# Feed-forward products of a two-layer decoder step: from one product in seven parts to both, with the squares kept in DRAM

## The chip, the cores and the metric

One core of a Trainium2 chip runs the whole program. The metric is the device time of one launch in microseconds (us), the median over the runs.

## The reference

Two layers work on 1056 tokens (1024 of a prompt, 32 of eight sampled sequences) with model width 1024. Layer 0 mixes tokens with a gated product over chunks of 128 positions, layer 1 with a sparse attention (an indexer, the top keys of each query, softmax). Each layer ends with a feed-forward net (FFN) of width 4096:

```python
def sqrelu_mlp(h, w1, w2):
    a = jax.nn.relu(h @ w1)
    return (a * a) @ w2
...
        xp = xp + op
        xs = xs + os_
        xp = xp + sqrelu_mlp(rms_norm(xp, norm_ffn[i]), ffn_w1[i], ffn_w2[i])
        xs = xs + sqrelu_mlp(rms_norm(xs, norm_ffn[i]), ffn_w1[i], ffn_w2[i])
```

In `dsa_sample`, each of the eight sequences attends to 1024 cached keys, gathered by pages, and to its own four new ones.

## The kernel before

Every fp32 operand is kept as two reduced fp32 parts, high and low, and every product is three matmuls: high by high, high by low, low by high (`mm3`, lines L242 to L248). `split` (L203, L204) makes the parts: ScalarE rounds the high one, VectorE (or GpSimd, where `lo_w` says so) subtracts for the low one. A scheduler places the instructions on each engine in advance; tiles come from pools whose `bufs` says how many buffers a name turns over.

The mixer ends with `out_proj`, which adds a product to the residual `X`, held in SBUF for the whole FFN (L500), and writes the scaled and split input of the FFN into the hidden state `h0`, `h1`, `h2` (L206, L207), chunk by chunk of 384, 384 and 288 tokens.

The FFN goes through the 4096 hidden columns in 16 blocks of 256. The first product of a block is plain: two weight tiles, each 24 matmuls for each of the three chunks. VectorE applies relu and the norm's factor (L526), ScalarE squares (L539). The second product takes tokens in two pairs of quarters (264 tokens each) and forms a 2 by 2 by 2 block product with seven products instead of eight: GpSimd adds and subtracts the squared hidden quarters (`combine0`, `combine1`, L550 to L558) and the weight blocks (L568 to L571), `split` makes `A2` and `w`, and `w2_pair` runs seven products for each of four output pairs and both token pairs, 168 matmuls of 264 columns for a block (L590 to L592). Every product is added into `X` at once, on VectorE from PSUM, and for one of the seven on GpSimd through a copy (L603, L581). The last of the 16 blocks uses a plain second product, and adds into `X` at L643.

The order follows this: `ffn` emits the first product of the next block between the four output pairs of the current one, and the scheduler keeps TensorE supplied from both.

## Time and profile before

| what | value |
|---|---|
| median of 3 runs | 2438.83 us (2437.76 to 2439.71) |
| the profiled execution | 2439.28 us, of it a span of 2436.9 us |
| granted TensorE clock, mean | 0.982 |
| TensorE busy | 2336.8 us, 96% of the span |
| VectorE, ScalarE, GpSimd busy | 69%, 44%, 54% |
| bytes moved by DMA | 158.38 MB, mean 65 GB/s |

Busy time of TensorE is the time in which a matmul is under way, and matmuls overlap; the spacing of their starts tells how fast it runs. A group's idle time is what its engine waited ahead of it, followed by what ended most of that wait.

### The profile page before, as it was taken

The numbers are of one execution on the slowest core, as the hardware profiler recorded it, in microseconds if no ns is written. First come the engines' busy times: TensorE is split into PE (matmuls) and PEld (weight loads), VectorE is DVE, ScalarE is ACT, GpSimd is POOL, SyncE is SP. The second block draws the span as 40 slices with busy tenths as digits, with TensorE's granted clock in tenths as the row PEclk, the third lists the DMA queues.
The fourth block names the chain that finished last, engine by engine and source line by source line (L and its number), as shares of the span: only waits on it lengthen the run. The fifth ranks groups of instructions, "written<-read, shape, count | busy, mean of one in ns | idle before, by whom it ended". The sixth has DMA issues, their size and how long they took to land.

```text
span 2436.9 us, 42780 instructions
## 1 busy us (share of the span) xinstructions
PE 2336.8 (96%) x15961; PEld 2246.2 (92%) x15961; DVE 1692.9 (69%) x3732; ACT 1062.5 (44%) x2164; POOL 1310.4 (54%) x1695
## 2 busy tenths in 40 slices
PE   8999999999999999989988968999999999999998
PEld 7999999999999999988988747899999999999998
DVE  6151257777777777774998879735677777777775
ACT  6232243333333333355865767734333333333335
POOL 2245446676676676561224435414566766766754
PEclk9999999999999999999999979999999999999999
DMA  6211301111111111141223441040111111111111
GB/s 231 61 46 35 123 27 46 47 48 49 44 48 48 49 52 40 55 131 30 84 70 104 142 173 27 10 158 27 44 48 45 48 49 45 51 46 49 53 44 72
DMA packets 180800, 158.38 MB, mean 65 GB/s; under 512 B 10376, under 2 KB 169712, under 8 KB 179568
## 3 DMA queue, kind: packets, MB, share of 16 engines
q1 hardware_dynamic: 176496, 136.78, 18.0%
q0 software_dynamic: 4096, 18.88, 2.3%
q8 instruction: 125, 2.05, 0.4%
q14 instruction: 83, 0.68, 0.1%
HBM read 134.15 MB, written 21.47 MB: 64 GB/s over the span
## 4 chain that ended last, share of the span: by engine, by line
PE 35%; DVE 9%; POOL 4%; issue 4%; ACT 2%; DMA 1%; SPq 0%; another core or an unknown queue 0%; DVEq 0%; POOLq 0%; ACTq 0%
PE ps L242 4%; PE ps L248 4%; PE ps L247 3%; PE px L242 3%; PE px L248 3%; PE px L247 3%; PE ps L590 2%; PE ps L591 1%; PE ps L592 1%; DVE sc L895 1%; POOL st L558 1%; PE pt L1138 1%; PE pt L592 1%; PE pt L591 1%; PE pt L590 1%
## 5 line engine op out<-in xcount | busy, mean ns | idle before, releaser
L581 POOL TENSOR_TENSOR X<-X,scr 128x264 f32<-128x264 f32 x480 | 427.0, 913 | 165.0 <-DVE X L581 119.4
L248 PE MATMUL ps<-h,w 128*128 128x384 f32 (+1 forms) x1344 | 438.3, 326 | 1.6 <-POOL w L204 1.4
L242 PE MATMUL ps<-h,w 128*128 128x384 f32 (+1 forms) x1344 | 437.1, 325 | 0.7 <-DVE scr L909 0.4
L247 PE MATMUL ps<-h,w 128*128 128x384 f32 (+1 forms) x1344 | 435.8, 324 | 0.0
L203 ACT ACTIVATE w<-raw 128x1024 fp32r<-128x1024 f32 (+2 forms) x248 | 250.6, 1012 | 305.6 <-PE px L247 123.3
L204 DVE TENSOR_TENSOR w<-raw,w 128x1024 fp32r<-128x1024 f32 (+1 forms) x211 | 298.4, 1414 | 32.9 <-ACT w L203 32.6
L242 PE MATMUL px<-h,w 128*128 128x384 f32 (+1 forms) x960 | 310.8, 324 | 0.3
L248 PE MATMUL px<-h,w 128*128 128x384 f32 (+1 forms) x960 | 309.8, 323 | 0.0
L247 PE MATMUL px<-h,w 128*128 128x384 f32 (+1 forms) x960 | 309.2, 322 | 0.0
L603 ACT ACTIVATE scr<-ps 128x264 f32<-128x264 f32 x240 | 92.7, 386 | 426.4 <-PE ps L592 380.3
L248 PEld LDWEIGHTS ps<-h,w 128*128 128x128 f32 x1344 | 254.4, 189 | 3.1 <-POOL w L204 1.7
L242 PEld LDWEIGHTS ps<-h,w 128*128 128x128 f32 x1344 | 254.6, 189 | 2.4 <-ACT w L203 1.0
L247 PEld LDWEIGHTS ps<-h,w 128*128 128x128 f32 x1344 | 254.4, 189 | 0.6
L581 DVE TENSOR_TENSOR X<-X,ps 128x264 f32<-128x264 f32 x480 | 197.4, 422 | 64.3 <-PE ps L592 64.3
L581 DVE TENSOR_TENSOR X<-X,px 128x264 f32<-128x264 f32 x480 | 194.2, 422 | 52.2 <-PE px L592 52.2
L581 DVE TENSOR_TENSOR X<-X,pt 128x264 f32<-128x264 f32 x480 | 203.1, 423 | 33.7 <-PE pt L592 29.0
L590 PE MATMUL ps<-A,w 128*128 128x264 f32 x720 | 206.8, 288 | 20.2 <-ACT A L203 20.2
L591 PE MATMUL ps<-A,w 128*128 128x264 f32 x720 | 206.6, 290 | 7.6 <-DVE A L204 7.5
L592 PE MATMUL ps<-A,w 128*128 128x264 f32 x720 | 203.6, 284 | 0.0
L568 POOL TENSOR_TENSOR raw<-raw 128x128 f32<-128x128 f32 x120 | 56.6, 472 | 267.7 <-DMA raw<-in_ffn_w 178.1
L204 DVE TENSOR_TENSOR A<-st,A 128x264 fp32r<-128x264 f32 (+2 forms) x184 | 164.1, 905 | 45.7 <-ACT A L203 45.6
L242 PEld LDWEIGHTS px<-h,w 128*128 128x128 f32 x960 | 180.4, 188 | 1.3 <-DVE X L581 1.2
...
## 6 DMA issues: line engine op xcount, KB each, us to landing
...
```

Of the source, the lines that this page charges most:

```text
L203: S.activation(hi, src, AF.Copy)
L204: (lo_w[0] or V).tensor_tensor(lo, src, f(hi), op=ALU.subtract)
L242: PE.matmul(out, lh, rh, start=first, stop=False)
L247: PE.matmul(out, lh, rl, start=False, stop=False)
L248: PE.matmul(out, ll, rh, start=False, stop=last)
L558: G.tensor_tensor(q[:, 1], q[:, 2], q[:, 1], op=ALU.subtract)
L568: G.tensor_tensor(sm[0], a21, a22, op=ALU.add)
L581: eng.tensor_tensor(x, x, src, op=op)
L590: PE.matmul(p, wh, xh, start=first, stop=False, skip_group_check=not first)
L591: PE.matmul(p, wh, xl, start=False, stop=False, skip_group_check=not first)
L592: PE.matmul(p, wl, xh, start=False, stop=True, skip_group_check=not first)
L603: S.activation(u, p, AF.Copy)
```

## The change

Both products of the FFN use the seven-product scheme, over eight blocks of 512 hidden columns (`NB`), in two phases. `out_proj` no longer keeps `X`: it streams rows of the residual from DRAM and back, and writes the scaled input into `XG`, in two halves of 528 tokens. `combos` makes and splits seven combinations of each half (14 in all) into slots that take the memory of the closed hidden state. Phase 1 runs 16 steps (`fb`, `kk`) of 168 matmuls of 264 columns; `summed` puts the outputs into a tile `h` (ScalarE writes four, VectorE adds four for each half), and `squares` applies relu, squares, makes the combinations for the second product, and stores 1.08 MB to DRAM (`hd`) for each half. Phase 2 reads them back (`hidden`), and for each of 8 blocks and four output pairs `m` runs 84 matmuls of 264 columns; the sums of 7 blocks go to the residual in DRAM by an accumulating DMA on GpSimd's queue, those of the last block into rows read back. The sample attention handles four sequences at a time for its softmax and masks from PSUM, without a copy of the mask.

```diff
+    def out_proj(w, gain, pre, x_in, x_out):
+        sx = [ExitStack() for _ in range(3)]
+        XG = [None, pool("x1", sx[1]).tile([P, NK, TH], F32, name="xg1")]
+        XG[0] = pool("x0", sx[0]).tile([P, NK, TH], F32, name="xg0")
+        rp = pool("xr", sx[2])
...
+            rows[d] = rp.tile([P, T], F32, name="row", bufs=3)
...
+            x = rows[o][:, sl]
+            V.tensor_tensor(x, p, x, op=ALU.add)
+            sumsq(x, o, sl)
+            for pr in range(2):
+                a, b = max(sl.start, pr * TH), min(sl.stop, (pr + 1) * TH)
+                if a < b:
+                    S.activation(XG[pr][:, o, a - pr * TH:b - pr * TH], rows[o][:, a:b], AF.Copy, scale=gain[:, o:o + 1])
+            if c == NC - 1:
+                SP.dma_start(x_out[o // 2][o % 2], rows[o])
...
+    def wino(nk, wt, xt, pr, post):
+        banks = {}
+        for key, first in PRODS:
+            if first:
+                banks[key[0]] = ps({"u": "ps", "v": "px"}.get(key[0], "pt"))
+            p = banks[key[0]][:, :SN]
+            kw = dict(skip_group_check=not first)
+            for k in range(nk):
+                wh, wl, xh, xl = wt(key, 0, k), wt(key, 1, k), xt(key, pr, 0, k), xt(key, pr, 1, k)
+                PE.matmul(p, wh, xh, start=first and k == 0, stop=False, **kw)
+                PE.matmul(p, wh, xl, start=False, stop=False, **kw)
+                PE.matmul(p, wl, xh, start=False, stop=k == nk - 1, **kw)
+            post(key, p)
+            yield
...
+    def run(*blocks):
+        for _ in PRODS:
+            for g in blocks:
+                next(g)
...
+    def summed(outs, add=False):
...
+        def start(p, q, op=ALU.add):
+            if add:
+                V.tensor_tensor(outs[q], outs[q], p, op=op)
+            else:
+                S.activation(outs[q], p, AF.Copy)
...
+        def post(key, p):
+            if key == "v5":
+                start(p, 3)
+            elif key == "u1":
+                start(p, 0)
+            elif key == "v3":
+                v3.append(p)
+            elif key == "u6":
+                start(p, 1)
+                V.tensor_tensor(outs[1], v3[0], outs[1], op=ALU.add)
+            elif key == "q4":
+                start(p, 2, ALU.subtract)
+            elif key == "p2":
+                V.tensor_tensor(outs[0], p, outs[0], op=ALU.add)
+            else:
+                V.tensor_tensor(outs[2], p, outs[2], op=ALU.add if add else ALU.subtract)
+                V.tensor_tensor(outs[3], p, outs[3], op=ALU.add)
+        return post
...
+    def w_sums(sm, a11, a21, a12, a22):
+        s1, s2, s4, s3 = sm
+        G.tensor_tensor(s1, a21, a22, op=ALU.add)
+        G.tensor_tensor(s2, s1, a11, op=ALU.subtract)
+        G.tensor_tensor(s4, a12, s2, op=ALU.subtract)
+        G.tensor_tensor(s3, a11, a21, op=ALU.subtract)
...
+    def w1_block(w1, fb, kk):
+        r = [raw([P, 2, 4, P]) for _ in range(2)]
+        for h in range(2):
+            for z in range(2):
+                c0 = fb * 512 + z * 256 + kk * P
+                SP.dma_start(r[h][:, z], w1[h * 512:(h + 1) * 512, c0:c0 + P].rearrange("(k p) f -> p k f", p=P))
...
+        sm = [raw([P, 2, 4, P]) for _ in range(2)]
+        s1, s2, s4, s3 = (sm[z // 2][:, z % 2] for z in range(4))
+        w_sums((s1, s2, s4, s3), a11, a21, a12, a22)
+        wt = {}
+        for key, src in (("v5", s1), ("u1", a11), ("v3", s4), ("u6", s2), ("q4", a22), ("p2", a12), ("u7", s3)):
+            wt[key] = wslot([P, 2, 4, P])
+            split(wt[key][:, 0], wt[key][:, 1], src)
+        return lambda key, z, k: wt[key][:, z, k]
...
+    def w2_block(w2, fb, m):
+        r, sm = raw([P, 2, 2, 2, P]), raw([P, 4, 2, P])
+        for h in range(2):
+            for z in range(2):
+                r0, c0 = fb * 512 + h * 256, m * 256 + z * P
+                SP.dma_start(r[:, h, z], w2[r0:r0 + 256, c0:c0 + P].rearrange("(k p) f -> p k f", p=P))
+        w_sums([sm[:, z] for z in range(4)], *(r[:, z // 2, z % 2] for z in range(4)))
+        wt = {}
+        for keys, src in ((("v5", "u6"), sm[:, 0:2]), (("u1",), r[:, 0, 0:1]), (("v3", "u7"), sm[:, 2:4]),
+                          (("p2", "q4"), r[:, 1])):
+            t = wslot([P, 2, 2, 2, P])
+            split(t[:, 0, :len(keys)], t[:, 1, :len(keys)], src)
+            for z, key in enumerate(keys):
+                wt[key] = t[:, :, z]
+        return lambda key, z, k: wt[key][:, z, k]
+    def ffn(layer, XG, sx, x_acc, done, keep):
...
+        def combos(pr, homes):
+            b11, b12, b21, b22 = (XG[pr][:, 4 * i:4 * i + 4, j * SN:(j + 1) * SN] for i in range(2) for j in range(2))
+            t1, t2, t3, t4 = (raw([P, 4, SN]) for _ in range(4))
+            def put(key, src, eng=None):
+                t = HC[pr][key] = homes[key]([P, 2, 4, SN])
+                lo_w[0] = eng
+                split(t[:, 0], t[:, 1], src)
+                lo_w[0] = None
...
+            put("v5", t1)
+            put("u1", b11)
+            put("v3", b22, G)
+            V.tensor_tensor(t3, b22, b12, op=ALU.subtract)
+            V.tensor_tensor(t2, t3, b11, op=ALU.add)
+            put("u6", t2)
+            V.tensor_tensor(t4, t2, b21, op=ALU.subtract)
+            put("q4", t4)
+            put("p2", b21, G)
+            put("u7", t3)
...
+        def squares(h, fb, kk, pr):
+            c = h[:, 0:4].rearrange("p (i j) t -> p i (j t)", i=2)
+            rb = rbc[:, None, pr * TH:(pr + 1) * TH].to_broadcast([P, 2, TH])
+            V.scalar_tensor_tensor(c, c, 0.0, rb, op0=ALU.max, op1=ALU.mult)
+            S.activation(c, c, AF.Square)
+            G.tensor_tensor(h[:, 4:8:2], h[:, 1:4:2], h[:, 0:2], op=ALU.subtract)
+            G.tensor_tensor(h[:, 5], h[:, 6], h[:, 0], op=ALU.add)
+            G.tensor_tensor(h[:, 7], h[:, 5], h[:, 2], op=ALU.subtract)
+            SP.dma_start(hd[fb][:, :, kk, pr].rearrange("j p t -> p j t"), h)
...
+        for fb in range(NB):
+            for kk in range(2):
+                wt = w1_block(w1, fb, kk)
+                hh = [fp.tile([P, 8, SN], F32, name="h", bufs=2) for _ in range(2)]
+                blocks = [wino(4, wt, xt1, pr, summed([hh[pr][:, q] for q in range(4)])) for pr in range(2)]
+                if fb == kk == 0:
...
+        def hidden(fb, some):
+            for key in some:
+                t = A2[fb, key] = homes[fb % 2][key]([P, 2, 2, 2, SN])
+                r = raw([P, 2, 2, SN])
+                SP.dma_start(r, hd[fb][HID[key]])
+                split(t[:, 0], t[:, 1], r)
...
+        for fb in range(NB - 1):
+            for m in range(4):
+                wt = w2_block(w2, fb, m)
+                out = fp.tile([P, 2, T], F32, name="out", bufs=2)
+                run(*(block(fb, m, pr, wt, out) for pr in range(2)))
+                G.dma_start(out=x_acc[m].rearrange("o p t -> p o t"), in_=out, accum_op=ALU.add)
...
+            wt = w2_block(w2, fb, m)
+            fetch(m)
+            run(*(block(fb, m, pr, wt, X[m], True) for pr in range(2)))
+            for i in range(2):
+                done(X, 2 * m + i, slice(0, T), c8)
+        wts = {m: w2_block(w2, fb, m) for m in (2, 3)}
...
+    def sample_softmax(z):
+        sel = cst("sel")[SB, z * P:(z + 1) * P]
+        mx = bl.tile([P, 3], F32, name="mxs", bufs=2)
...
+            V.tensor_tensor_reduce(out=SS[z][:, c0:c1], in0=p[:, :c1 - c0], in1=SS[z][:, c0:c1], scale=-ATTN_SCALE,
+                                   scalar=mx[:, i - 1:i] if i else 3.4e38, op0=ALU.add, op1=ALU.min,
+                                   accum_out=mx[:, i:i + 1])
...
+            vgs.append(c8([P, 2048], F32))
...
-    sample_mask()
-    for kv in range(2):
-        sample_softmax(kv)
```

In the sample attention the score dots move into each sequence's key loop, the mask product is made for each group of four and added straight from PSUM, and the values are gathered into the FFN's slots before the softmax.

The scheduler's order shows what this moves. First, ScalarE where layer 0's FFN begins: before, the last rows are the scaled input of the last chunk (`h2`) with the weights `w` among them, and then the first squares (`st`).

```order
L206 ACTIVATE h2_71<-X_2516,gains_78 128x288 [waits PE_49] x3
L203 ACTIVATE w_3584<-raw_3578 128x1024 [waits DMAHW3_49,PE_49]
L299 ACTIVATE scr_3320<-X_2516 128x288 [waits DVE_49,Pool_49]
L206 ACTIVATE h2_71<-X_2516,gains_78 128x288 [waits PE_49]
L539 ACTIVATE st_3391<-scr_3389 128x264 [waits DVE_49]
```

The same place of the changed kernel, ScalarE: `c` are the split combinations (the last one made ahead is `c_3455`), `w` the first weights of phase 1.

```order
L220 ACTIVATE c_3416<-raw_3399 128x1056 [waits DVE_49,PE_49]
L220 ACTIVATE c_3419<-xg0_2536 128x1056 [waits Activation_49]
L220 ACTIVATE c_3422<-raw_3398 128x1056
...
L220 ACTIVATE c_3449<-raw_3432 128x1056 [waits DVE_49]
L220 ACTIVATE c_3452<-xg1_2532 128x1056
L220 ACTIVATE c_3455<-raw_3431 128x1056
L220 ACTIVATE w_3474<-raw_3468 128x512 [waits Pool_49]
L220 ACTIVATE w_3477<-raw_3462 128x512 [waits DMAHW7_49]
```

All 14 splits of combinations stand before the first weight, and the first of them waits for TensorE. VectorE's rows have the same order: 10 low parts ahead of `w_3474`.

Second, GpSimd in the middle of phase 1, changed kernel: L682 to L684 are the combinations of the squares in a tile `h`, L600 to L603 the sums of weight blocks.

```order
L682 TENSOR_TENSOR h_4929<-h_4929 128x2x264 [waits DMAHW3_49,Activation_49]
L602 TENSOR_TENSOR raw_5381<-raw_5375,raw_5380 128x512 [waits DMAHW4_49,DVE_49]
L603 TENSOR_TENSOR raw_5381<-raw_5374 128x512
L683 TENSOR_TENSOR h_4929<-h_4929 128x264 [waits Pool_49]
L684 TENSOR_TENSOR h_4929<-h_4929 128x264 [waits Pool_49]
L600 TENSOR_TENSOR raw_5619<-raw_5613,raw_5614 128x512 [waits DMAHW3_49,DMAHW0_49,DVE_49]
L682 TENSOR_TENSOR h_4930<-h_4930 128x2x264 [waits DMAHW6_49,Activation_49]
L601 TENSOR_TENSOR raw_5619<-raw_5619,raw_5613 128x512 [waits DMAHW7_49,Pool_49]
L683 TENSOR_TENSOR h_4930<-h_4930 128x264 [waits Pool_49]
L684 TENSOR_TENSOR h_4930<-h_4930 128x264 [waits Pool_49]
```

Sums of weights stand between the combinations of a tile, which its store to DRAM waits for. ScalarE then starts the next tile of that half with a row that waits for that store (a DMA):

```order
L577 ACTIVATE h_5168<-px_5170 128x264 [waits DMAHW1_49,Activation_49,Pool_49]
L577 ACTIVATE h_5168<-ps_5198 128x264
L577 ACTIVATE h_5168<-pt_5278 128x264
L681 ACTIVATE h_4930<-h_4930 128x1056 [waits DVE_49]
L577 ACTIVATE h_5168<-ps_5198 128x264 [waits PE_49]
```

Third, ScalarE in phase 2, changed kernel: `out` is the tile of sums, which L727 on GpSimd's queue accumulates into DRAM. The first write of a tile waits for that DMA (DMASW) of the tile two back.

```order
L577 ACTIVATE out_7631<-px_7632 128x264 [waits DMASW0_49,DVE_49,PE_49]
L577 ACTIVATE out_7631<-px_7640 128x264 [waits PE_49]
L577 ACTIVATE out_7631<-ps_7648 128x264 [waits PE_49]
L220 ACTIVATE w_7770<-raw_7751 128x512 [waits DMAHW3_49,DMAHW2_49,PE_49]
L577 ACTIVATE out_7631<-ps_7656 128x264 [waits PE_49]
```

The wait is on the accumulate of `out_7347`, issued at L727, two tiles earlier.

## Rows read from the trace of the kernel before

**Rows 1.** The page, part 1: busy time of each engine.

```profile
PE 2336.8 (96%) x15961; PEld 2246.2 (92%) x15961; DVE 1692.9 (69%) x3732; ACT 1062.5 (44%) x2164; POOL 1310.4 (54%) x1695
```

**Rows 2.** Windows: two stretches; busy time and count by engine, granted clock, DMA share, GB/s.

```profile
341.00:1040.00 699.00, 684.57 (x4822) 677.76 (x4822) 526.92 (x1039) 254.02 (x525) 452.72 (x593) 1.00 0.16 47
...
1695.00:2437.00 742.00, 720.79 (x5074) 713.53 (x5072) 549.81 (x1086) 282.36 (x584) 473.28 (x619) 1.00 0.16 49
```

**Rows 3.** One line's instructions, with the first and the last start.

```profile
L500 DVE TENSOR_TENSOR X<-ps,X x24: 444/548/559, 263.8 to 1694.9; 128x384 f32<-128x384 f32 x16, 128x288 f32<-128x288 f32 x8
...
L653 SPq DMA_DIRECT2D xd<-X x24: 319/320/731, 1046.2 to 1074.0; - x24
...
L643 DVE TENSOR_TENSOR X<-px,X x24: 442/545/558, 1045.7 to 2424.3; 128x384 f32<-128x384 f32 x16, 128x288 f32<-128x288 f32 x8
```

**Rows 4.** Timeline of TensorE in layer 1: start, length, line, operation.

```profile
1866.82 0.29 PE L590 MATMUL pt<-A,w 128*128 128x264 f32 x1
...
1867.91 0.34 PE L242 MATMUL ps<-h,w 128*128 128x384 f32 x1
1868.09 0.34 PE L247 MATMUL ps<-h,w 128*128 128x384 f32 x1
```

**Rows 5.** The chain that ended last, layer 1: start, length, what.

```profile
1857.72 1.71 POOL st L556
...
1902.83 1.71 POOL st L556
```

**Rows 6.** Groups by line and shape: count, busy us, mean ns, idle before.

```profile
L203 ACT ACTIVATE w<-raw 128x1024 fp32r<-128x1024 f32 x220 | 233.1, 1060 | 290.0 <-PE px L247 123.3 <-PE ps L591 72.2 <-POOL raw L571 37.5
L204 DVE TENSOR_TENSOR w<-raw,w 128x1024 fp32r<-128x1024 f32 x203 | 290.5, 1431 | 32.9 <-ACT w L203 32.6 <-issue 0.3
L204 POOL TENSOR_TENSOR w<-raw,w 128x1024 fp32r<-128x1024 f32 x17 | 41.7, 2458 | 83.9 <-ACT w L203 83.9
L204 POOL TENSOR_TENSOR w<-raw,w 128x512 fp32r<-128x512 f32 x20 | 26.2, 1320 | 77.5 <-ACT w L203 69.5 <-DVE idh L470 7.8
L204 DVE TENSOR_TENSOR raw<-pt,raw 128x512 fp32r<-128x512 f32 x76 | 51.6, 685 | 24.4 <-ACT raw L203 16.7 <-PE px L247 5.9 <-issue 1.7
L603 ACT ACTIVATE scr<-ps 128x264 f32<-128x264 f32 x240 | 92.7, 386 | 426.4 <-PE ps L592 380.3 <-POOL X L581 46.1
L581 DVE TENSOR_TENSOR X<-X,px 128x264 f32<-128x264 f32 x480 | 194.2, 422 | 52.2 <-PE px L592 52.2
L413 DVE SCALAR_TENSOR_TENSOR GV<-GV,mv,gain_bc 128x1024 f32<-128x1024 f32 x8 | 10.2, 1277 | 0.0
```

**Rows 7.** Timelines of GpSimd and VectorE, 1811 to 1814 us.

```profile
1811.85 0.76 POOL L558 TENSOR_TENSOR st<-st 128x264 f32<-128x264 f32 x1
1812.56 1.75 POOL L556 TENSOR_TENSOR st<-st 128x264 f32<-128x264 f32 x1
...
1811.75 0.76 DVE L581 TENSOR_TENSOR X<-X,px 128x264 f32<-128x264 f32 x2
1812.43 1.26 DVE L204 TENSOR_TENSOR w<-raw,w 128x1024 fp32r<-128x1024 f32 x1
```

**Rows 8.** DMA issues: count, median us from issue to landing.

```profile
raw<-in_cache_k,idh POOLq DMA_INDIRECT x16, 5.2
...
h<-in_cache_v,idh POOLq DMA_INDIRECT x8, 6.2
```

**Rows 9.** Timeline of TensorE, sample attention.

```profile
1406.18 0.28 PE L247 MATMUL px<-KT,t 128*128 128x256 f32 x1
1406.30 0.28 PE L248 MATMUL px<-KT,t 128*128 128x256 f32 x1
...
1410.22 0.58 PE L242 MATMUL px<-KT,t 128*128 128x256 f32 x1 [3.41 <-DVE mx L1125]
1410.59 0.42 PE L247 MATMUL px<-KT,t 128*128 128x256 f32 x1
1410.81 0.41 PE L242 MATMUL px<-KT,t 128*128 128x256 f32 x1
```

435 lines of the change are left out of this document (185 added, 250 removed).

## The prediction

> **What bounds the kernel now.** I read the page's busy times first: TensorE is busy 96% of the span, the other engines 44% to 69% [rows 1], so what counts is how many matmuls there are, how long one takes, and where TensorE waits. The windows give the stage: in 699 us of layer 0's FFN TensorE is busy 684.6 us, in layer 1's 742 us with the tail 720.8 us, at full clock both times, with DMA at 0.16 of its engines [rows 2]. The FFN of layer 0 lasts from about 341 to 1074 us, 733 us; that of layer 1 from 1694.9 to the last add at 2424.3, with the add itself about 729.5 us [rows 3]. Together 1462 of 2439 us.
>
> For the price of a matmul, the spacing of starts serves, not the length shown, since matmuls overlap: nine of 264 columns take 1867.91 - 1866.82 = 1.09 us, 0.121 us each, and one of 384 columns 0.18 (0.455 ns a column) [rows 4]. A block of 256 hidden columns has 144 matmuls of 352 columns on average (0.160 us) and 168 of 264: 23.0 + 20.3 = 43.4 us. The chain of waits passes the same GpSimd sum every 45.1 us [rows 5], so a block waits some 1.7 us, 26 us over a layer.
>
> **What the change saves.** Before, a layer has 2304 first-product matmuls (368.6 us), 2520 of the seven-product kind (304.9) and 144 in the plain last block (23): 696.5 us. After, 16 steps of 168 and 32 of 84 of 264 columns make 5376 x 0.121 = 650.5 us. So 46 us a layer of matmuls go, and with them the 26 of waits; everything else is what comes in their place.
>
> **Entry into the FFN.** Before, TensorE runs on without a gap, since chunks of the hidden state are scaled and split one by one. In the order, 14 splits of 1056 columns stand on ScalarE and 10 on VectorE, with three sums, before the first weight, and the first waits for the last matmul of the projection, whose memory it takes. ScalarE: 14 x 1.09 (1060 ns for 1024 columns) = 15.3 us. VectorE: 13 x 1.45 = 18.9, and 0.7 for the weight. GpSimd: four splits of 2.46 and four weight sums of 1.32 = 15.1 [rows 6]. Side by side 20 to 22 us. TensorE is slower after a wait: two matmuls of 256 columns that follow 3.41 us of idling are 0.22 us apart, before it 0.12 [rows 9]; I add 2. I take **24 us** a layer; 17 if ScalarE alone sets it, 35 if VectorE and GpSimd go one after the other.
>
> **Phase 1, 16 steps.** TensorE's floor is 20.3 us. Each half has one buffer of `h`, so a step of the second half is a loop. From the end of its last product: 0.35 to VectorE, two adds of 0.38, one split of 512 columns ahead (0.69), relu with the factor on 1056 columns (1.28 us for 1024), the square on ScalarE (1.1) [rows 6], GpSimd's 528 + 264 + 264 columns with one weight sum of 512 between (1.4 + 0.75 + 0.75 + 1.32, from 0.75 us for 264 [rows 7] and 1.32 for 512 [rows 6]) = 4.2, then the store of 1.08 MB, the copy that waited for it (0.39), and 60 matmuls (7.3) until that half's last product ends again. The trace has no store of this size to DRAM; bounds are 3.7 us (1.08 MB at the FFN's 47 GB/s over a DMA share of 0.16, 294 GB/s [rows 2]) and 6.2 us, the landing of the gathers of 1.05 MB on another queue [rows 8]. I take 5.4, nearer the second, which has a start and an end in it. Sum: **21.5 us**, bounds 20.3 and 22.3; 16 of them 344.
>
> Going to phase 2, the first hidden tile must be loaded and split into slots that phase 1 frees with its last products: one landing of 0.5 MB is 5.2 us [rows 8]; I take **5 us**, between 0 (all pulled ahead) and 8 (with a split after it).
>
> **Phase 2, 28 steps.** The floor is 84 x 0.121 = 10.16 us. VectorE has eight adds (3.4), weight splits and hidden splits, about 9 us, ScalarE 7, GpSimd 4 to 5, so no engine alone is over the floor. An `out` tile is written, accumulated, and free for the step after next: 11.3 us from its first copy to its last product (a step and the products pulled ahead), 1 us for the last adds, then the accumulate. The trace has no accumulating DMA. It cannot be under one plain landing, 6.2 us for 1.05 MB [rows 8], and reading the destination adds bytes: 3.7 us for each further pass, one pass 9.9, two 13.6 if nothing overlaps. I take 9.0, a second pass that overlaps in part. The loop: 11.3 + 1 + 9.0 = 21.3 for two steps, **10.65** each; bounds 10.16 and 12.95. 28 of them: 298.2.
>
> **Rest.** The last block is four steps of 10.16 and 3 us of adds: 43.6 us. In the sample attention the mask copies go and one product is made twice; TensorE waits there anyway (3.41 us on VectorE in one place [rows 9]), and I take -5 us, between -10 and +5. The rows that the projection streams and the wider constants lie beside work that TensorE covers; uncovered, the last row store would add one landing, 6 us, to a layer.
>
> **The sum.** A layer: 24 + 344 + 5 + 298.2 + 43.6 = 714.8 us; two 1429.6 against 1462. With -5 for attention it is 37 less than the profiled execution's 2439.3, whose median over the runs is 0.5 lower: **2402 us**. The likeliest case's own range is 2365 to 2445: 0.6 us on each of 32 steps and 0.35 on each of 56.
>
> **A shared path of VectorE and GpSimd.** The row: a GpSimd sum of 264 columns takes 0.76 us beside VectorE's adds from PSUM, and 1.75 us when a VectorE split with both inputs in SBUF runs (1.26 us) from just before it [rows 7]. In the changed phase 1 four GpSimd rows of the loop stand where VectorE does seven weight splits of 0.69 and two relu passes a step. If in the middle they wait 1.9 us in all, the step is 23.4 instead of 21.5, and the time 2402 + 32 x 1.9 = 2463. The Trainium skill, "SBUF — State Buffer", section "Who interferes with whom", states that a VectorE instruction with two SBUF inputs contends with a GpSimd instruction that reads SBUF, as an exclusive lock; by that rule 2463 is the time, and on the one pair of rows the trace agrees. I keep the lower one as likelier since GpSimd's loop rows come when VectorE's splits for the next step are partly done.
>
> **Rivals.**
> 1. *TensorE stays fed.* Steps of 20.5 and 10.25 us: the store and the accumulate fit behind the products that the scheduler pulled ahead. For it: DMA is at 0.16 now, so there is room. Against: the order's rows wait for the store and the accumulate by name. Layer 24 + 328 + 5 + 287 + 43.6 = 687.6; time about **2348**.
> 2. *The accumulate sets phase 2* (slower). If reading and writing the residual are passes one after the other, 13.6 us instead of 9.0, the loop is 25.9 us, 12.95 a step, 2.3 more on 56 steps: **2531**. It decides from an accumulate of about 10.3 us on, where 0.66 us a step eat the 37. For it: two gathers of the same queue land at 5.2 and 6.2 us [rows 8], so most of the price of one is fixed, and a second pass may be fixed again. Against: the fixed parts may overlap over 16 engines.
> 3. *GpSimd behind VectorE in phase 1* (slower), as worked out: **2463**.
> 4. *The saving is eaten by the entries.* VectorE and GpSimd in turn, 35 us instead of 24, and the row store uncovered, 6: 34 more, **2436**, no change.
>
> **Chances.** Forecast 0.36, rival 1 0.20, rival 2 0.20, rival 3 0.17, rival 4 0.07. Within 0.2% (5 us, about what a measurement of this kernel can tell from no change) lie part of the forecast's upper end and half of rival 4: 0.06. Faster 0.20 + 0.32 + 0.01 = 0.53, slower 0.41. The range holds all but 2 in 10: from 2345 (rival 1 without all its entry) to 2555 (rival 2 with a little of rival 3).
>
> **What would show it.** In the changed profile: TensorE idle for 17 to 35 us at each FFN entry, with the split of a weight as what ends it; in phase 1 the first copy into `h` coming every 21 to 22 us, TensorE's wait ended by ScalarE's copy; in phase 2 steps of 10.65 us, and GpSimd's accumulates landing 9 us after issue. Right or wrong is told apart by the lengths of the two phases, 344 and 298 us a layer. I am wrong if the accumulate lands after 12 us or more, if GpSimd's sums of 264 columns are mostly near 1.75 us, or if steps are at TensorE's floor.

## The result and the profile after

The changed kernel takes **2864.36 us** (median of 4 runs, 2858.51 to 2867.77) against 2438.49 us: ratio 1.174, 95% interval 1.172 to 1.176, 426 us slower. It lies outside the range given, and on the other side of the forecast. The profiled execution takes 2867.77 us, its span is 2866.0.

The page of the changed kernel: busy times, DMA queues and DMA issues:

```profile
PE 2388.0 (83%) x16817; PEld 2269.6 (79%) x16817; DVE 1635.3 (57%) x3070; ACT 1245.3 (43%) x2495; POOL 1141.4 (40%) x1143
...
q0 software_dynamic: 19328, 79.44, 13.9%
...
xa<-out POOLq DMA_DIRECT2D x28, 1056.0 KB, 10.9
xe<-out POOLq DMA_DIRECT2D x28, 1056.0 KB, 11.1
```

TensorE is busy 83% of the span where it was 96% [rows 1]; its busy time rose from 2337 to 2388 us, although there is less matmul work; one reason is that a matmul that follows a wait takes longer (0.59 us at 1001.17 in the rows below, 0.29 at 995.90). Bytes by DMA went from 158 to 366 MB, and the packets of GpSimd's queue (`q0`) take 13.9% of the 16 DMA engines' time. The time from the issue of a DMA until its data have arrived is called its landing here; it is the last number of the two lower lines.

Lines with first and last start give the stages: the projection's residual adds (L529), the last block's adds (L575) and the issues of the accumulating DMAs, called accumulates (L727):

```profile
L529 DVE TENSOR_TENSOR row<-ps,row x24: 440/554/559, 261.4 to 1972.1; 128x384 f32<-128x384 f32 x16, 128x288 f32<-128x288 f32 x8
...
L575 DVE TENSOR_TENSOR out<-out,pt x8: 415/420/430, 1187.1 to 1236.9; 128x264 f32<-128x264 f32 x8
L575 DVE TENSOR_TENSOR c<-c,ps x16: 416/420/430, 2805.3 to 2848.8; 128x264 f32<-128x264 f32 x16
...
L727 POOL DMA_DIRECT2D xa<-out x28: 1179/1196/1377, 791.4 to 1174.5; - x28
L727 POOL DMA_DIRECT2D xe<-out x28: 1179/1200/1364, 2419.5 to 2804.1; - x28
```

| stage | before | forecast | after |
|---|---|---|---|
| start to the end of layer 0's projection | 340 | 340 | 351 |
| FFN of layer 0 | 733 | 715 | 886 |
| attention and its projection | 621 | 616 | 735 |
| FFN of layer 1 | 729.5 | 715 | 877 |

The before column of the third row is the time between the stages in [rows 3]; layer 0's projection ends at 351.3 in the timeline of the changed kernel, and the other limits are the rows above (L529 at 1972.1 to its end, L575 at 1236.9 and 2848.8). The stages of the changed kernel sum to 2849 us, and 17 us follow them (12 before).

Windows of 100 us, in phase 1 and in phase 2 (length; busy time and count of TensorE, its weight loads, VectorE, ScalarE and GpSimd; granted clock, DMA share, GB/s):

```profile
500.00:600.00 100.00, 92.17 (x742) 90.54 (x741) 56.48 (x77) 38.87 (x76) 52.41 (x45) 1.00 0.46 143
...
900.00:1000.00 100.00, 79.68 (x588) 77.97 (x588) 59.61 (x95) 44.47 (x97) 37.67 (x35) 0.93 0.77 182
```

In phase 1 TensorE runs 742 matmuls in 100 us; in phase 2 588, with DMA at 0.77 of its engines and a granted clock of 0.93. In the attention, from 1700 to 1800 us, VectorE is busy 96 of 100 us and TensorE 34. Three of the longest sums among TensorE's waits (sum, count, longest):

```profile
PE px L558 <- ACT out L577: 153.3, 49, 6.4
PE px L558 <- ACT h L577: 73.3, 40, 4.6
PE pt L301 <- DVE dg L300: 54.8, 11, 17.4
```

These are the first copies into `out` (phase 2) and into `h` (phase 1), and the product that spreads the norm's factor, which waits longest at the entries into the FFN. The fourth, in the attention, is one wait, in the timeline:

```profile
1806.84 0.74 PE L259 MATMUL px<-KT,t 128*128 128x448 f32 x1 [67.45 <-DVE mx L1230]
```

**Phase 2.** The accumulates of layer 0 are (1174.5 - 791.4) / 27 = 14.19 us apart, those of layer 1 14.24; forecast 10.65, floor 10.16. The timelines of ScalarE, VectorE, GpSimd and TensorE over one step, engine by engine:

```profile
985.54 0.39 ACT L577 ACTIVATE out<-px 128x264 f32<-128x264 f32 x1 [4.73 <-DMA xa<-out]
1000.73 0.39 ACT L577 ACTIVATE out<-px 128x264 f32<-128x264 f32 x1 [6.18 <-DMA xa<-out]
...
1001.95 0.76 DVE L221 TENSOR_TENSOR w<-raw,w 128x512 fp32r<-128x512 f32 x1 [4.88 <-ACT w L220]
1002.63 0.42 DVE L594 TENSOR_TENSOR out<-ps,out 128x264 f32<-128x264 f32 x1
1002.98 0.42 DVE L595 TENSOR_TENSOR out<-ps,out 128x264 f32<-128x264 f32 x1
...
1003.38 1.77 POOL L601 TENSOR_TENSOR raw<-raw 128x256 f32<-128x256 f32 x1
1005.10 1.20 POOL L727 DMA_DIRECT2D xa<-out  x1
...
995.90 0.29 PE L560 MATMUL ps<-c,w 128*128 128x264 f32 x1
...
1001.17 0.59 PE L558 MATMUL px<-c,w 128*128 128x264 f32 x1 [4.26 <-ACT out L577]
```

The tile whose first copy ran at 985.54 (`out_9462` below) gets its last adds (L594, L595) at 1002.63 and 1002.98, although TensorE had ended the product for them by 996.2 (the row of 995.90). The order of the changed kernel's instructions at this place shows why so late. On ScalarE, the copy into the next tile, which waits for the landing of an accumulate (`DMASW6_49`), and behind it the first part of a split of weights:

```
L577 ACTIVATE out_9599<-px_9600 128x264 [waits DMASW6_49,DVE_49,PE_49]
L577 ACTIVATE out_9599<-ps_9616 128x264 [waits PE_49]
L220 ACTIVATE w_9735<-raw_9720 128x512 [waits PE_49,Activation_49,Pool_49]
```

and on VectorE the second part of that split ahead of the adds of the tile before:

```
L221 TENSOR_TENSOR w_9735<-raw_9720,w_9735 128x512 [waits DVE_49,Activation_49]
L594 TENSOR_TENSOR out_9462<-ps_9487,out_9462 128x264 [waits PE_49]
L595 TENSOR_TENSOR out_9462<-ps_9487,out_9462 128x264
```

ScalarE stands 6.18 us at the copy (1000.73), VectorE behind it at a split, the adds behind that, and the accumulate of the finished tile goes out at 1005.10, behind one more weight sum on GpSimd. The tile took 1002.98 - 985.54 + 0.42 = 17.9 us from first copy to last add, and 1.7 more to its accumulate, where the forecast had 11.3 + 1 = 12.3 and nothing. So here the landing of one tile holds the end of the other, and two buffers do not let two steps overlap. Of the 53 steps with a tile before and one after, 34 end with a tile whose last adds stand behind such a split in the order of instructions; these took 15.5 us on the mean, the other 19 took 12.1.

**Attention.** The counting of the top-k, by group (`sma`, `smc` on ScalarE, `smb`, `smd` on VectorE), first and last start; before:

```profile
L700 DVE TENSOR_SCALAR_CACHE_REDUCE junkb<-sc,smb x62: 599/673/746, 1178.6 to 1322.7; 128x384 int8<-128x384 f32 x31, 128x512 int8<-128x512 f32 x31
L721 ACT ACTIVATE junkc<-sc,smc x62: 812/901/997, 1233.1 to 1436.8; 128x640 int8<-128x640 f32 x31, 128x768 int8<-128x768 f32 x31
L700 DVE TENSOR_SCALAR_CACHE_REDUCE junkd<-sc,smd x62: 1111/1198/1280, 1301.7 to 1460.9; 128x896 int8<-128x896 f32 x31, 128x1024 int8<-128x1024 f32 x31
```

and after:

```profile
L821 DVE TENSOR_SCALAR_CACHE_REDUCE junk<-sc,smb x62: 599/673/747, 1396.4 to 1509.6; 128x384 int8<-128x384 f32 x31, 128x512 int8<-128x512 f32 x31
L842 ACT ACTIVATE junk<-sc,smc x62: 812/898/987, 1513.3 to 1665.3; 128x640 int8<-128x640 f32 x31, 128x768 int8<-128x768 f32 x31
L821 DVE TENSOR_SCALAR_CACHE_REDUCE junk<-sc,smd x62: 1117/1199/1280, 1672.0 to 1797.6; 128x896 int8<-128x896 f32 x31, 128x1024 int8<-128x1024 f32 x31
```

Before, the three run beside each other (1179 to 1323, 1233 to 1437, 1302 to 1461). After, they run one after another: 1396 to 1510, 1513 to 1665, 1672 to 1798. Each group before had its own scratch tile for the compared values (`junkb`, `junkc`, `junkd`); the change shares two, one written by VectorE's counts and one by ScalarE's. A ScalarE group begins and ends with one count on VectorE, which writes VectorE's scratch tile: so it starts after the VectorE group before it, and the next VectorE group comes after its end.

### The profile page after: what moved, and what is told of

Read it like the earlier page. It is cut to its first block, busy times and chain, and to the rows that moved or that the text cites. A ratio compares the mean times of both kernels' runs of the same rounds, so it can differ in the third digit from the quotient of the medians.

```text
span 2866.0 us, 44250 instructions
## 1 busy us (share of the span) xinstructions
PE 2388.0 (83%) x16817; PEld 2269.6 (79%) x16817; DVE 1635.3 (57%) x3070; ACT 1245.3 (43%) x2495; POOL 1141.4 (40%) x1143
## 3 DMA queue, kind: packets, MB, share of 16 engines
q0 software_dynamic: 19328, 79.44, 13.9%
## 5 line engine op out<-in xcount | busy, mean ns | idle before, releaser
L221 DVE TENSOR_TENSOR w<-raw,w 128x256 fp32r<-128x256 f32 (+3 forms) x503 | 460.8, 930 | 261.9 <-ACT w L220 256.9
L558 PE MATMUL px<-c,w 128*128 128x264 f32 x1024 | 322.9, 316 | 250.7 <-ACT out L577 153.3
L220 ACT ACTIVATE w<-raw 128x512 fp32r<-128x512 f32 (+3 forms) x540 | 335.3, 630 | 372.5 <-PE px L560 126.5
L558 PE MATMUL ps<-c,w 128*128 128x264 f32 x1536 | 451.4, 296 | 4.5 <-ACT out L577 3.7
L559 PE MATMUL ps<-c,w 128*128 128x264 f32 x1536 | 452.2, 295 | 0.0
L560 PE MATMUL ps<-c,w 128*128 128x264 f32 x1536 | 449.5, 294 | 0.1
L558 PEld LDWEIGHTS px<-c,w 128*128 128x128 f32 x1024 | 211.5, 207 | 271.8 <-ACT out L577 163.9
L560 PE MATMUL px<-c,w 128*128 128x264 f32 x1024 | 310.2, 304 | 1.5 <-DVE w L221 1.5
L559 PE MATMUL px<-c,w 128*128 128x264 f32 x1024 | 311.3, 304 | 0.0
L558 PEld LDWEIGHTS ps<-c,w 128*128 128x128 f32 x1536 | 306.6, 201 | 6.0 <-ACT out L577 4.4
L559 PEld LDWEIGHTS ps<-c,w 128*128 128x128 f32 x1536 | 306.7, 200 | 0.0
L560 PEld LDWEIGHTS ps<-c,w 128*128 128x128 f32 x1536 | 304.7, 199 | 0.7 <-DVE w L221 0.7
L558 PE MATMUL pt<-c,w 128*128 128x264 f32 x1024 | 299.5, 293 | 0.8 <-DVE out L592 0.5
L559 PE MATMUL pt<-c,w 128*128 128x264 f32 x1024 | 298.1, 291 | 0.0
L560 PE MATMUL pt<-c,w 128*128 128x264 f32 x1024 | 297.8, 291 | 0.3 <-DVE w L221 0.3
L221 DVE TENSOR_TENSOR c<-raw,c 128x1056 fp32r<-128x1056 f32 x128 | 190.1, 1498 | 119.5 <-ACT c L220 119.0
L600 POOL TENSOR_TENSOR raw<-raw 128x256 f32<-128x256 f32 (+1 forms) x96 | 107.8, 1123 | 351.8 <-DMA raw<-in_ffn_w 221.1
L560 PEld LDWEIGHTS px<-c,w 128*128 128x128 f32 x1024 | 212.7, 208 | 1.9 <-DVE w L221 1.9
L559 PEld LDWEIGHTS px<-c,w 128*128 128x128 f32 x1024 | 213.1, 208 | 0.0
L603 POOL TENSOR_TENSOR raw<-raw 128x256 f32<-128x256 f32 (+1 forms) x96 | 110.3, 1149 | 250.0 <-DMA raw<-in_ffn_w 225.5
L558 PEld LDWEIGHTS pt<-c,w 128*128 128x128 f32 x1024 | 200.7, 196 | 2.1 <-ACT out L577 1.2
L559 PEld LDWEIGHTS pt<-c,w 128*128 128x128 f32 x1024 | 200.4, 196 | 0.0
```

Of the source, the lines that this page charges most:

```text
L220: S.activation(hi, src, AF.Copy)
L221: (lo_w[0] or V).tensor_tensor(lo, src, f(hi), op=ALU.subtract)
L558: PE.matmul(p, wh, xh, start=first and k == 0, stop=False, **kw)
L559: PE.matmul(p, wh, xl, start=False, stop=False, **kw)
L560: PE.matmul(p, wl, xh, start=False, stop=k == nk - 1, **kw)
L600: G.tensor_tensor(s1, a21, a22, op=ALU.add)
```

## Experiments

Theories for the attention: A, the shared scratch tiles make it longer; B, its new order does. For phase 2: C, a step is a landing and then a tail, the work from the landing to the next accumulate's issue; D, the DMA engines or the queue are simply full. E and F are for the entry, G and H for phase 1's loop. Later, for what puts landing and tail in turn: Q, the queues of ScalarE, VectorE and GpSimd; T, TensorE's order. Where one time is given, the kernel ran once; beside these runs the kernel before took 2434 to 2442 us. Four times of one version lie 9 to 23 us apart, so smaller differences of single times say nothing.

**e1, scratch by kind of group.**

```diff
-        junk_v, junk_a = junks
+        junk_v = junk_a = junks[how == "act"]
```

> The changed kernel, with the two shared int8 scratch tiles of the top-k split between the groups by kind (one for the groups counted on VectorE, one for the groups counted on ScalarE) instead of by engine. Theory A, the shared tile makes the last top-k group on VectorE wait for the end of the group before it on ScalarE: the attention stage gets back some 90 to 115 us, about 2750 to 2775 us in all, and the 67 us wait of TensorE for VectorE goes. Theory B, the stage is longer because of the sample attention's new order and work: no more than 15 us change, 2850 or more.

2775.8 us, 89 less, which is A, at the edge of its range. The groups overlap again:

```profile
L821 DVE TENSOR_SCALAR_CACHE_REDUCE junk<-sc,smd x62: 1131/1200/1282, 1491.1 to 1637.2; 128x896 int8<-128x896 f32 x31, 128x1024 int8<-128x1024 f32 x31
```

**e2, the kernel before with shared scratch.**

```diff
+    junks = [tkp.tile([P, L_S], I8, name="junk%d" % z) for z in range(2)]
...
-        junk = tkp.tile([P, max(x.shape[1] for x in blocks)], I8, name="junk" + tag)
+        junk_v, junk_a = junks
...
```

> The kernel before, with only this part of the change: the scratch tiles of the top-k shared by all groups, one for VectorE's counts and one for ScalarE's. Theory A: slower by 80 to 115 us, 2520 to 2555. Theory B: within 10 us of 2438.

2551.99 us, 112 more than before, at the upper end of A's range. TensorE's waits show the same 67.4 us, where its longest for this cause was 3.41 [rows 9]:

```profile
PE px L242 <- DVE mx L1127: 103.4, 12, 67.4
```

A is shown from both sides: sharing that saves 1.3 KB of a partition's memory costs 89 to 112 us, in either kernel; e1 shares two tiles as well and does not pay it. B keeps what is left of the 114, some 14 us with the row-wise projection (698 us from the last accumulate to the projection's last add in e1, 798 in the changed kernel).

**e3, plain store.**

```diff
-                G.dma_start(out=x_acc[m].rearrange("o p t -> p o t"), in_=out, accum_op=ALU.add)
+                G.dma_start(out=x_acc[m].rearrange("o p t -> p o t"), in_=out)
```

> The changed kernel, with a plain store in place of the accumulating one in phase 2; this leaves out the adding of the blocks' sums to the residual. Theory C, a phase 2 step is one landing of the accumulate (11 us) plus the tail of the products (some 3.5 us): the plain store lands after 6 to 7 us, the steps fall from 14.2 to about 10.3 to 10.8 us, about 2655 to 2680 us in all. Theory D, phase 2 is bound by something that a plain store has too (queue, bytes, weights arriving late): steps stay at 13 us or more, 2795 or more.

2668.88 us. Steps of 11.10 us in layer 0 and 10.69 in layer 1; the landing falls to 6.2 and 7.2, the issue from 1.2 to 0.74 us:

```profile
L727 POOL DMA_DIRECT2D xa<-out x28: 719/742/928, 786.7 to 1086.3; - x28
...
xa<-out POOLq DMA_DIRECT2D x28, 1056.0 KB, 6.2
xe<-out POOLq DMA_DIRECT2D x28, 1056.0 KB, 7.2
```

The time lies in C's range and far from D's; the steps lie at C's upper end and above it. They are near TensorE's floor of 10.16, so this run does not show that a landing still sets them. The DMA engines' time shows what the accumulate itself costs: `q0` 13.9% of 2866 is 398 us, less the gathers' 56 us (2.3% of 2437 before, taken as unchanged) 342, or 6.1 us for each of 56 accumulates; with the plain store 8.3% of 2667, 2.95 us each. The accumulate takes twice the engines' time.

**e4, output tiles of 528 tokens.**

```diff
-                out = fp.tile([P, 2, T], F32, name="out", bufs=2)
+                out = [fp.tile([P, 2, TH], F32, name="out%d" % pr, bufs=2) for pr in range(2)]
...
-                G.dma_start(out=x_acc[m].rearrange("o p t -> p o t"), in_=out, accum_op=ALU.add)
+                for pr in range(2):
+                    G.dma_start(out=x_acc[m].rearrange("o p t -> p o t")[:, :, pr * TH:(pr + 1) * TH], in_=out[pr],
+                                accum_op=ALU.add)
...
```

> The changed kernel, with the output tile of phase 2 cut into two tiles of 528 tokens, each with its own accumulate and two buffers of its own; same bytes. Theory C: the first half's accumulate starts earlier and each has half the bytes, so the wait of a step shrinks; steps of 10.8 to 12 us, about 2665 to 2740 in all. Theory D, the DMA engines are full and the bytes decide: steps of 13.5 us or more, 2820 or more.

2759.45 us, 105 less with the same bytes, which D did not allow. Half an accumulate lands after 8.6 and 8.1 us, and 27.5 steps take 342.6 us, 12.46 each (12.15 in layer 1); steps and time are a little above C's ranges. The window 800 to 1060 us, of this kernel:

```profile
800.00:1060.00 260.00, 227.53 (x1715) 222.75 (x1714) 170.43 (x280) 129.06 (x280) 121.07 (x121) 0.94 0.90 200
```

DMA is now at 0.90: 12.46 x 0.90 = 11.2 us of all engines a step, above TensorE's 10.16 (the changed kernel: 0.76 of the same window, 0.76 x 14.19 = 10.8). If busy time is taken as work, an estimate, D is not the first limit but the second, and it lies close behind.

**e5, a third output tile, and e6, its control.** To make room, e5 has three staging buffers (`raw`) for weights and hidden tiles instead of five; e6 has that alone.

```diff
+        raw_bufs(3)
         sf = ExitStack()
         fp = pool("fc", sf)
...
-                out = fp.tile([P, 2, T], F32, name="out", bufs=2)
+                out = fp.tile([P, 2, T], F32, name="out", bufs=3)
...
```

> The changed kernel, with three output tiles in phase 2 instead of two, and, to make room, three staging buffers for weights and hidden tiles in phase 2 instead of five; the accumulates and their bytes stay. Theory C, a step waits for the accumulate of two tiles back, whose own last products stand behind the wait of the tile between: with a third tile the wait goes, steps of 10.3 to 12 us, 2640 to 2745 us in all. Theory D, the DMA engines' bytes or the queue decide: steps stay at 13.5 us or more, 2825 or more. If fewer staging buffers cost more than the tile gives, the next run tells.

> Control of the run before: the changed kernel with two output tiles, and three staging buffers in phase 2 instead of five. If the staging buffers matter little, within 20 us of 2864; if weights or hidden tiles then arrive late, 40 us more or worse.

2813.23 and 2843.21 us. C's ranges are missed: the tile takes 30 us off, and steps stay at 13.6 in e5, as D had it, and 13.8 in e6; e5's time is 12 us under D's. TensorE's waits of e6 and then e5:

```profile
PE px L558 <- ACT out L577: 109.6, 44, 5.4
...
PE px L558 <- ACT w L220: 38.5, 19, 7.6
```

```profile
PE px L558 <- ACT w L220: 75.3, 39, 7.1
...
PE px L558 <- ACT out L577: 36.8, 22, 4.0
PE ps L558 <- ACT out L577: 21.2, 18, 3.3
```

The wait for tiles halves, from 110 to 58 us, and the wait for weights doubles. With three staging buffers weights come late, so this pair says that the tiles matter, and not how much they would with five. That fewer staging buffers make the changed kernel 21 us faster was not expected; its accumulates land 9.7 and 9.3 us after issue, instead of 11. Why is not shown.

**e7, weights between the halves.**

```diff
+        w00 = w1_block(w1, 0, 0)
         combos(1, dict(zip(keys, [c2] * 2 + [c8] * 5)))
...
+                wt = w00 if fb == kk == 0 else w1_block(w1, fb, kk)
```

> The changed kernel, with the first weights of phase 1 loaded and split between the combinations of the first token half and those of the second, instead of after both. Theory E, the entry is the 14 splits and 10 low parts in a row ahead of the weights: TensorE starts some 8 to 14 us earlier in each layer, 2836 to 2850. Rival F, the entry is set by what the first half alone needs and GpSimd's share: within 8 us of 2864.

2868.20 us: F by its time. TensorE begins phase 1 at 359.0 instead of 379.5 us, and then stops again, as its timeline shows:

```profile
359.04 0.59 PE L558 MATMUL px<-c,w 128*128 128x264 f32 x1 [1.75 <-ACT w L220]
366.74 0.59 PE L560 MATMUL px<-c,w 128*128 128x264 f32 x1 [6.37 <-DVE w L221]
```

It waits for VectorE's splits one by one. From 351 to 382 us VectorE is busy 30.3 of 31 us here and 29.7 in the changed kernel, ScalarE 16.6 and 16.2: VectorE's work fills the entry, and this change of its order does not shorten it.

**e8 and e9, the weight sums of phase 1.** e8 leaves them out and splits loaded blocks in their place; e9 makes them on VectorE:

```diff
...
-        w_sums((s1, s2, s4, s3), a11, a21, a12, a22)
+        w_sums((s1, s2, s4, s3), a11, a21, a12, a22, V)
```

> The changed kernel, with GpSimd's four sums of weight blocks in phase 1 left out (raw blocks are used in their place, so the FFN's first product is another one). Theory G, in phase 1 the sums stand between the combinations of the squares and lengthen the loop of a tile through GpSimd and the store: steps of 22.5 us fall to 20.5 to 21.3, 2805 to 2835 in all. Rival H, the store to DRAM and VectorE's share of the loop are enough to hold it: steps of 22 us or more, 2850 or more.

> The changed kernel, with the four sums of weight blocks of phase 1 on VectorE instead of GpSimd; same result. Theory G (the sums on GpSimd stand in the loop of a tile): steps of 20.8 to 21.8 us instead of 22.5, 2810 to 2845 in all. Rival: VectorE, which has two passes of its own in that loop, delays it as much as GpSimd did, 2855 or more.

2794.35 and 2798.74 us: 70 and 66 less, more than G expected, with steps as G had them; H and the rival of e9 fall. The window 540 to 700 us, of the changed kernel, e8 and e9:

```profile
540.00:700.00 160.00, 148.68 (x1194) 145.81 (x1193) 88.23 (x121) 61.59 (x119) 81.49 (x73) 1.00 0.46 142
```

```profile
540.00:700.00 160.00, 155.85 (x1273) 155.00 (x1272) 86.32 (x128) 64.80 (x127) 48.74 (x46) 1.00 0.49 153
```

```profile
540.00:700.00 160.00, 155.52 (x1262) 153.66 (x1261) 106.09 (x155) 64.05 (x125) 48.90 (x45) 1.00 0.51 155
```

1194, 1273 and 1262 matmuls in 160 us are steps of 22.5, 21.1 and 21.3 us (168 matmuls each). From the first to the last store of a half the gain is larger: a step takes 23.4 us in layer 0 and 24.0 in layer 1, in e8 21.9 and 22.0, in e9 22.1 and 21.6. VectorE takes over four two-input instructions a step and still the loop is shorter. In phase 1 TensorE waits for copies into `h` (34.6 and 38.7 us) and hardly for weights, so what the sums held was GpSimd's queue between the square and the store. One half's turn there, changed kernel:

```profile
635.55 1.32 POOL L682 TENSOR_TENSOR h<-h 128x528 f32<-128x528 f32 x1 [2.71 <-ACT h L681]
637.49 1.28 POOL L602 TENSOR_TENSOR raw<-raw 128x512 f32<-128x512 f32 x1 [0.63 <-DVE w L221]
638.73 1.29 POOL L603 TENSOR_TENSOR raw<-raw 128x512 f32<-128x512 f32 x1
...
641.26 1.09 POOL L684 TENSOR_TENSOR h<-h 128x264 f32<-128x264 f32 x1
```

Two sums stand between the combinations, and a wait of 0.63 us before them.

**e10, the three repairs together** (e1, e4, e9).

> The changed kernel with the top-k's scratch tiles split by kind, output tiles of 528 tokens in phase 2, and the weight sums of phase 1 on VectorE, together; same result. If the three causes are separate, the gains add: 90, 105 and 20 to 55, 2615 to 2650 us. If they share a cause, 2690 or more. In neither case below the kernel before.

2584.88 us (median of 4, 2574.69 to 2597.29), 1.061 times the kernel before (1.056 to 1.065): 279 less, where 89, 105 and 66 make 260. The gains add, so the causes are separate; the range was missed since it had 20 to 55 for e9, and 20 us on top of the sum are not explained. It is slower than before.

**e11, half tiles with plain stores, and e12, all repairs with plain stores.**

> The changed kernel with output tiles of 528 tokens and plain stores instead of accumulating ones, which leaves out the adding of the blocks' sums to the residual. If the DMA engines' time for the accumulate is what keeps the half tiles at 12.5 us a step, steps of 10.2 to 10.6 us, 2630 to 2655 in all; if the tiles' waits are, 11.1 us as with whole tiles and plain stores, 2665 or more.

> The repaired kernel with plain stores instead of accumulating ones, which leaves out the adding of the blocks' sums to the residual. If the accumulate is the largest cost that is left, some 90 to 115 us go, 2470 to 2495; what then stays above the kernel before (30 to 55 us) would be the entries into the FFN and the passage to phase 2. If the accumulate is now hidden, 2560 or more.

2650.94 us, with 27.5 steps in 293.3 us, 10.67 each: the first case by its time, the steps a little above its 10.2 to 10.6. Against a plain store the accumulate costs (12.46 - 10.67) x 56 = 100 us of the 108 between e4 and e11. e12 took 2497.24 us, 88 less than e10, 2 above its range, and 55 above the kernel before beside it: even with plain stores the scheme does not reach it.

**e13, phase 2's splits on VectorE, and e14, the first copies on VectorE.** The edit of e13, and then of e14:

```diff
-            S.activation(hi, src, AF.Copy)
+            if hi_v[0]:
+                V.tensor_copy(hi, src)
+            else:
+                S.activation(hi, src, AF.Copy)
...
+        hi_v[0] = True
         hidden(0, keys)
...
```

```diff
-            if add:
+            if add == "copy":
+                V.tensor_copy(outs[q], p)
+            elif add:
...
-                run(*(block(fb, m, pr, wt, out) for pr in range(2)))
+                run(*(block(fb, m, pr, wt, out, "copy") for pr in range(2)))
```

> In phase 2 VectorE makes both parts of every split (weights and squares, the first part too), so ScalarE does nothing there but the first copies into the output tiles. The order of the built program then has, at 50 of 55 tiles, nothing of VectorE that stands ahead of a tile's last adds and waits for ScalarE behind its copy into the next tile; in the changed kernel it is so at only 19 of 55, and the step that ends with such a tile takes 12.1 us there, against 15.5 us at the others. Theory Q (the queues: ScalarE's waiting copy holds its splits, these hold VectorE's queue and so the last adds): a step falls to 11.4 to 13.0 us, not lower since VectorE takes over some 4 us of ScalarE's work and has 8.2 us of its own; 2700 to 2795 us. Theory T (TensorE's order: products for the next tile stand ahead of the last ones of this tile): nothing of TensorE's own changes, a step stays at 13.8 to 14.5, 2840 to 2880 us.

> The other way about: the first copies into the output tiles are made by VectorE instead of ScalarE, the splits stay as they are. The copy that waits for a landing now stands in VectorE's own queue, ahead of the tile's last adds at 52 of 55 tiles (36 of 55 are held in the changed kernel). Theory Q: nearly every step is one of the held kind, 15.5 us where that was seen, so 14.6 to 16.5 us a step and 2885 to 2995 us, although ScalarE has less to do. Theory T: the engine that copies does not matter, 13.8 to 14.5 us a step, 2840 to 2880 us.

2813.82 us with steps of 13.3 and 13.0, and 2842.43 us with 14.4 and 14.0: e13 falls between the theories, nearer to Q. In e14 Q's range is missed and T's holds, though T's for e13 is missed. So the count of tiles whose last adds are held, though it parts slow steps from quick ones in the changed kernel, does not set the mean by itself. The timelines of VectorE and GpSimd in e13 show a third queue:

```profile
997.96 0.41 DVE L599 TENSOR_TENSOR out<-ps,out 128x264 f32<-128x264 f32 x1
...
998.99 2.13 POOL L607 TENSOR_TENSOR raw<-raw 128x256 f32<-128x256 f32 x1 [8.66 <-DMA raw<-in_ffn_w]
1002.57 1.19 POOL L732 DMA_DIRECT2D xa<-out  x1
```

The last add is done at 998.4, and its accumulate goes out at 1002.57: GpSimd was at weight sums, the first of which had waited 8.66 us for a weight load.

**e16 and e17, without the sums of phase 2**, with e13's edit and alone:

```diff
-        w_sums([sm[:, z] for z in range(4)], *(r[:, z // 2, z % 2] for z in range(4)))
...
-        for keys, src in ((("v5", "u6"), sm[:, 0:2]), (("u1",), r[:, 0, 0:1]), (("v3", "u7"), sm[:, 2:4]),
+        for keys, src in ((("v5", "u6"), r[:, 1]), (("u1",), r[:, 0, 0:1]), (("v3", "u7"), r[:, 0]),
```

> e13 with GpSimd's weight sums of phase 2 left out (the splits read the loaded quarters in their place, so the output is another), so that GpSimd has only the accumulates there; two staging tiles a step become free with them. In e13 the adds of one tile were done at 997.96 us and its accumulate was issued at 1002.57, behind sums that had waited 8.66 us for a weight load. Theory Q (the queues hold the step, GpSimd's the last of them): the accumulate follows the adds at once, a step is 10.7 to 12.0 us where e13 has 13.2, 2680 to 2760 us. Theory C (a step is a landing and 3.2 to 4.4 us in turn, whatever stands in the queues; a landing took 9.7 us in e13): 12.4 to 13.6 us a step, 2770 to 2835 us.

> The sums of phase 2 left out as in e16, but the splits as in the changed kernel, with 35 of 55 tiles whose last adds stand behind a split that waits for ScalarE. Theory Q: one queue less, the other stays: 12.8 to 14.0 us a step, 2785 to 2860 us, and e16 lies under it by 1 to 2.5 us a step. Theory C: as in e16 within 0.5 us a step.

2738.08 and 2766.93 us. The accumulates of e16, by line:

```profile
L731 POOL DMA_DIRECT2D xa<-out x28: 1203/1203/1391, 797.0 to 1114.6; - x28
...
DMA to landing us min/median/max: 8.3/10.0/12.5
```

(1114.6 - 797.0) / 27 = 11.76 us a step, with a landing that still takes 10.0: C's 12.4 to 13.6 falls, and Q's range holds. e17 has 12.2 and 12.4: less than Q gave it, and only 0.6 above e16, where Q had 1 to 2.5. The sums are 1.9 us of the step, the splits on ScalarE another 0.6 once they are gone (1.0 where they are not, e13). Leaving the sums out also frees a staging tile of each step (`sm`; the text above counts two) and lets the splits start without GpSimd. How the 1.9 us divide between these and the wait of the accumulate in GpSimd's queue was not taken apart.

**e15, whole tiles with repairs** (e1, e9, e13), **and e18, e10 with phase 2's sums on VectorE.**

> Whole output tiles with accumulates, and three repairs: scratch by kind of group (89 us in e1), phase 1's weight sums on VectorE (66 us in e9), phase 2's splits on VectorE as in e13. Theory Q: 2864 less 155 less the 70 to 160 us of e13's case, 2550 to 2640 us, about what half tiles gave in e10 (2585). Theory T: 2695 to 2725 us.

> e10 with the weight sums of phase 2 on VectorE too, so that GpSimd makes no sums in either phase. In e10 a step took 12.36 and 11.57 us with the DMA engines busy 0.92 of the window 800 to 1060 us. Theory Q (GpSimd's sums hold the accumulates; without them e17's step fell by 1.9 us with whole tiles): 11.2 to 11.7 us a step, 2540 to 2570 us. Theory D2 (with half tiles the DMA engines are the limit: 12.36 x 0.92 = 11.4, and nothing of GpSimd counts): within 15 us of e10, 2570 to 2600 us. Neither reaches the kernel before.

2644.42 us (ratio 1.085, 1.083 to 1.087), 4 above Q's range, as e13 gave only 50; and 2604.37 us (1.069, 1.067 to 1.071), 20 more than e10 and 4 above D2's range: with half tiles GpSimd's sums are not what holds, and D2 is the nearer, with the DMA engines at 0.90 of the same window. e10 stays the fastest version of the change that accumulates.

## Why the prediction was wrong

The forecast missed the profiled execution by 466 us. By stages: some 195 us lie in the steps of phase 2, 119 in the attention, 90 in phase 1, the rest in passages and ends.

**Right:** the matmul count and price (5376 a layer, 0.122 us from start to start where TensorE does not wait), the places of the waits (the store before the copy into `h`, the accumulate before the copy into `out`, the entry), and that there is a gap at the entry.

**Entry, the term "Side by side 20 to 22 us".** Phase 1 starts 28 us after the projection's last add (351.3 to 379.5 in layer 0); forecast 24, bound 35. The longest wait, 17.4 us, is ended not by the split of a weight but by VectorE's `dg` for the norm's factor, which stands in its queue behind the splits of the combinations. VectorE is busy 29.4 of 30.7 us:

```profile
351.30:382.00 30.70, 6.85 (x29) 6.02 (x30) 29.42 (x24) 15.85 (x20) 22.15 (x11) 0.56 0.22 69
...
358.84 1.24 DVE L221 TENSOR_TENSOR c<-raw,c 128x1056 fp32r<-128x1056 f32 x1
361.18 3.49 DVE L221 TENSOR_TENSOR c<-xg,c 128x1056 fp32r<-128x1056 f32 x1
...
360.34 6.62 POOL L221 TENSOR_TENSOR c<-xg,c 128x1056 fp32r<-128x1056 f32 x2 [3.71 <-ACT c L220]
```

The same subtraction takes 1.24 us alone and 3.49 beside GpSimd's two (the last row): the two engines did not work side by side. That is rival 4's reason, at a part of its price.

**Phase 2, the step "The loop: 11.3 + 1 + 9.0 = 21.3 for two steps".** This is the step that failed, and where the sign was lost: 14.2 us a step instead of 10.65, 3.55 x 56 = 199 us. The accumulate lands after 11 us, 2 more than taken and within the bounds (6.2 to 13.6). The larger part is the 11.3 + 1 us of a tile from first copy to last add, which were taken from TensorE's work alone: they became 17.9, and 1.7 to the accumulate, in the step shown, since the copy that waits for the landing stands in ScalarE's queue ahead of splits, these in VectorE's ahead of the other tile's last adds, and weight sums in GpSimd's ahead of its accumulate. The forecast named what the copy waits for, and not what is queued behind it. With the landing at 11 in the form forecast, (11.3 + 1 + 11) / 2 = 11.65 a step would have come; without sums and splits in the way (e16) 11.7 came, with a landing of 10, for which the form gives 11.15. Rival 2 had the accumulate right as what sets phase 2, but with a dearer landing (13.6) and a bound of 12.95; the queues pass it with a cheaper one. The prediction also has no sum of the DMA engines' time in phase 2. By the estimate in e4 it is 10.8 us a step, and 0.88 of the same window x 11.76 = 10.3 in e16, so by this estimate 10.65 was about the least that the accumulating scheme could reach.

**Attention, the step "I take -5 us, between -10 and +5".** It came to +114. The term looked at the mask copies of the sample attention; the scratch tiles, which the change also makes shared and which tie two engines, were not priced. e1 and e2 give 89 and 112 us to them.

**Phase 1, the step "Sum: 21.5 us".** 22.5 in the middle of the phase, and 385 and 393 us for the two phases, where 344 was the sum: many of the other steps take 24 to 27 us. The store was near (5.4 forecast, 4.7 and 5.7 seen). Undersized was GpSimd's term, 4.2 us from the square to the store: it took 6.9 in the half shown with e9, and 5.2 in the other half of that step, since two weight sums stand in the way of each half, and one was counted. e8 and e9 give 1.2 to 1.4 us a step to the sums there, and 1.3 to 2.4 over the whole phase.

**The shared path of VectorE and GpSimd** (2463 by it). GpSimd's sums of 264 columns (L683) took 0.945 us on average here (0.76 in [rows 7]), so some contention is there, far from 1.75. The Trainium skill, "SBUF — State Buffer", section "Who interferes with whom", states that a VectorE instruction with two SBUF inputs contends with a GpSimd instruction that reads SBUF. The traces agree: e9 adds four such instructions to VectorE in each step, and the median of these sums rises from 0.775 to 1.08 us. Yet e9's step fell by 1.2 us, so this contention was not what held phase 1. Where the rows show it to count is the entry.

**Passage to phase 2, last block and start.** Some 17 us lie between phase 1's last products (764) and phase 2's first copies (781), 5 forecast. TensorE waits there 7.3 us for the first weights, which stand behind GpSimd's sums, and 6.4 us for the copy into `out`, whose tile takes the memory of `h` and waits for its last store. The last block of layer 0 takes 63 us from the last accumulate to the last add, 43.6 forecast; one add waits 10.4 us for residual rows to be read back. In layer 1 it is 45. The first stage is 11 us longer because TensorE, which did not wait there before, waits 4.4 us for a split by ScalarE, and 4.3 for two by GpSimd:

```profile
PE ps L259 <- ACT w L220: 4.4, 1, 4.4
```

What delays these splits was not tried. VectorE's wait for the first residual row, 16.6 us, is not it: the kernel before has one of 15.3.

What stays open: how the 55 us that e12 has over the kernel before divide. The entries (28 us each) and passages (some 16 us each) could account for them beside the saving of matmuls, but that was only argued.
